# Making the context's gated convolution channels one stage earlier, on other engines

## The chip, the core and the metric

The kernel runs on one core of one Trainium2 chip. The core's engines work from queues of their own and wait for each other by semaphores: TensorE (PE, matrix products, with PEld for its weight loads), VectorE (DVE), ScalarE (ACT), GpSimd (POOL) and SyncE (SP, which here issues the loads). The metric is the device time of one execution in microseconds, lower is better.

## The reference, cut to what matters

Two blocks follow each other. The first one (two layers) ends with a feed-forward layer and a norm. The second one begins with the even mixer, which takes two streams of 256 tokens and 1024 channels: the latent stream, which is the first block's output, and the context stream, which is an input and depends on nothing before it.

```
p = h @ w_in                     # both streams, 2560 columns
a, gate = p[..., :512], p[..., 512:1024]
u = depthwise_conv(a * sigmoid(gate), conv_w (31 taps), conv_b)
conv = silu(layer_norm(u, ln_g, ln_b))
q, k, v = the other columns of p; attention over the keys of both streams
y = concat([conv, attention]) @ w_out
first block's last step:  x = x + 0.5 * (silu(gate) * up) @ w_down,  then a norm
```

## The kernel before

Activations lie with channels on the 128 partitions and tokens along the free axis. Every product is made in three passes: weights and activations are split into a rounded high part and a low rest, and `mm3` (L639 to L641) multiplies high by high, high by low and low by high. Weights come from DRAM in chunks of six 128x128 blocks (`raw`, issued by SP at L405); ACT makes the high part (`whi`, L418) and DVE the low one (`wlo`, L419, which reads `raw` and `whi`). Four buffers each of `raw`, `whi` and `wlo` let this run ahead of PE by at most three chunks; blocks are consumed in the order in which they were packed.

The feed-forward layer ahead of the even mixer (`ffn`, name `ffn2_1`) makes 22 pairs of products of its hidden units (gate and up, 8 blocks each, L715 to L719, split by L449 and L450) and then 8 products of 22 blocks, each of which is added to `x` (L725, L726) and fed to the next norms (`feed`: L478, L491, L492, L499 to L503). A generator `context` is woven into it (0.8 steps for each step of the layer): it loads nothing large, but sums, normalises and splits the context stream (L502, L520 to L524), so that the context is ready for products before the mixer starts.

The mixer (`even`) starts with four channel groups `m`. For each, `linc` makes the products of both streams from one pass over the weights: context first (256 columns, evacuated by ACT alone, L681), then latent (258 columns; these need the norm's factor `R`, which two reciprocals at L623 give some microseconds later: L685 on DVE, then L687, L688 on ACT). The gated unit goes to `glu[m]`, a tile with both streams side by side (L1161). The convolution of a group is a generator of 31 taps (`taps`), each 128x512, both streams at once. On DVE a tap is one SCALAR_TENSOR_TENSOR (L1092) into PSUM (`ms`); for groups marked otherwise ACT scales the shifted tile into `z` (L1089) and POOL adds `z` to `conv` (L1090). `BY` gives the engine of each group: 0 is DVE, 1 is ACT and POOL, -14 gives 14 taps to DVE and 17 to ACT and POOL. `tap` is called after each stream's products and hands out as many taps as `TAPS` says (first pair of numbers while the gated units are made, second pair in k, v and q). The k, v and q products follow (4 groups each, with a rotation of the latent k and q by a small matmul, L1182 to L1186, and transposes of v, L1196), then the attention (scores L1236, maxima L1238, exponentials L1241, transposes L1254 and L1256, values L1259, merge L1268 to L1281), into which `EV_FILL` weaves the q products, the rest of the convolution, its layer norm (`conv_norm`, L1310 to L1339) and the first output products.

The order of each engine's queue is set by a scheduler when the program is built; `issue_after(s.mark)` says that a tap stands behind the marked ACT instruction. At run time each queue goes strictly in its order.

Of the kernel before, what the change touches and what calls it, by code (L numbers as in the profile page):

```python
# [17 lines left out]
F32 = mybir.dt.float32  # L18
# [5 lines left out]
P = 128  # L24
# [22 lines left out]
TAPS = ((4.0, 4.0), (2.0, 2.0))  # L47
BY = (0, 1, 0, -14)
# [58 lines left out]
def _ffn_blocks(gu, down, parts):  # L107
# [195 lines left out]
def _prep(i):  # L303
# [4 lines left out]
    for l in range(2):  # L308
        for w in (1, 2):
            a[f"w_ffn{w}_{l}"] = _pack(_ffn_blocks(i[f"ffn{w}_w_gu"][l], i[f"ffn{w}_w_down"][l], FFN_PARTS[w, l]))  # L310
            cols.add(f"ffn{w}_norm{l}", i[f"ffn{w}_norm"][l])
# [260 lines left out]
class Net:  # L572
# [128 lines left out]
    def ffn(s, name, nr, nxt, parts):  # L701
# [3 lines left out]
        with s.tc.tile_pool(name=name, bufs=1) as pool:  # L705
            n = max(len(hs) for hs in parts)
            h = Split(pool.tile([P, n, T], F32R, name="hh"), pool.tile([P, n, T], F32R, name="hl"))
            for hs in parts:
                for m in range(len(hs)):
# [361 lines left out]

    def even(s, nrs, pool, cat, nxts):
# [3 lines left out]
        W31 = 31  # L1076
        cw, cb = s.col("ev_conv_w"), s.col("ev_conv_b")
        us, convs, due, ends = [], {0: [], 1: []}, {0: 0.0, 1: 0.0}, []

        def taps(u, y, m, by, js, last):  # L1080

            acc = y if by else s.ms().rearrange("p (s t) -> p s t", s=2)
            for j in js:
                k, v = cw[:, m * W31 + j:m * W31 + j + 1], u[:, :, j:j + T]
                if j == js[0]:
                    nc.scalar.activation(acc, v, AF.Copy, scale=k)
                elif by:
                    z = pool.tile([P, 2, T], F32, tag="w8", name="z", bufs=8)
                    nc.scalar.activation(z, v, AF.Copy, scale=k)  # L1089
                    nc.gpsimd.tensor_tensor(y, y, z, op=ALU.add)  # L1090
                else:
                    nc.vector.scalar_tensor_tensor(acc, v, k, acc, op0=ALU.mult, op1=ALU.add)  # L1092
                if j == js[-1]:
                    ends.append([2, lambda: last(acc)])
                yield

        def halve(y, m, acc):
            nc.scalar.activation(y, acc, AF.Identity, scale=0.5, bias=cb[:, m:m + 1])

        total = []  # L1100

        def done(y):

            total.append(y)
            if len(total) == 2:
                t = pool.tile([P, 2, T], F32, tag="w8", name="total", bufs=8)
                eng = nc.vector if len(us) == 4 and not any(convs.values()) else nc.gpsimd
                eng.tensor_tensor(t, total[0], total[1], op=ALU.add)
                total[:] = [t]

        def convolve(m, u):
            y = u[:, :, :T] if BY[m] == 0 else pool.tile([P, 2, T], F32, name=f"conv{m}")
            us.append(y)
            if BY[m] in (0, 1):
                convs[BY[m]].append(taps(u, y, m, BY[m], range(W31), lambda acc: (halve(y, m, acc), done(y))))
                return

            n, parts = -BY[m], []

            def part(acc):  # L1120
                parts.append(acc)
                if len(parts) == 2:
                    v = next(a for a in parts if a is not y)
                    t = pool.tile([P, 2, T], F32, tag="w8", name="z", bufs=8)
                    halve(t, m, v)
                    nc.vector.scalar_tensor_tensor(y, y, 0.5, t, op0=ALU.mult, op1=ALU.add)
                    done(y)

            convs[0].append(taps(u, None, m, 0, range(n), part))
            convs[1].append(taps(u, y, m, 1, range(n, W31), part))  # L1130

# [15 lines left out]

        glu = [pool.tile([P, 2, T + W31 - 1], F32, name=f"glu{m}") for m in range(4)]
        for u in glu:
            nc.gpsimd.memset(u[:, :, :15], 0.0)  # L1150
            nc.gpsimd.memset(u[:, :, 15 + T:], 0.0)
        for m in range(4):
            pa, pg = s.linc(w, nrs), s.linc(w, nrs)
            u = glu[m]
            for st in pa:
                a, th = pa[st], s.tmp("t3")
                if not nrs[st].full:
                    a = s.tmp("t2")
                    s.scaled(a, pa[st], nrs[st])
                s.scaled(th, pg[st], nrs[st], AF.Tanh, 0.5)  # L1160
                nc.vector.scalar_tensor_tensor(u[:, st, 15:15 + T], th, 1.0, a, op0=ALU.add, op1=ALU.mult)  # L1161
                tap(TAPS[0])
            convolve(m, u)
            yield
# [59 lines left out]
        def attend(st):  # L1224
# [5 lines left out]
            def probs(b, h):  # L1230
                es, r = [], s.tmp("mx", 8, bufs=6)
                assert {("q", h), ("v", h)} <= ready
                for mp in range(2):
# [6 lines left out]
                    e = pool.tile([P, S], F32, tag="e1" if st else "w8", name="e", bufs=4 if st else 8)  # L1240
# [63 lines left out]
        def conv_norm():  # L1304
# [3 lines left out]
            wide = lambda: pool.tile([P, 2, T], F32, tag="w8", name="wide", bufs=8)  # L1308
# [715 lines left out]
    def first_block(s):  # L2024
# [36 lines left out]
        drain(weave(s.ffn("ffn2_1", nr, nx, FFN_PARTS[2, 1]), ctx, 0.8))  # L2061
        drain(ctx)
# [34 lines left out]
```

## Time and profile before

| what | value |
|---|---|
| median of 3 runs (range) | 2242.39 us (2240.51 to 2242.43) |
| the profiled execution: its own time, its span | 2243.55 us, 2241.8 us |
| PE, DVE, ACT, POOL busy, share of the span | 98%, 77%, 57%, 4% |
| last feed-forward layer, some 984 to 1170 us: PE busy | 186.0 of 186 us |
| even mixer up to the attention, 1170 to 1290 us: PE and DVE busy | 113.6 and 104.7 of 120 us |
| attention to the first output products, 1290 to 1400 us: PE and ACT busy | 99.4 and 79.9 of 110 us |

PE is close to always busy, so time is to be won only where a stretch shows fewer matmuls than PE can start; the windows by stretch are the place to look, and after them the chain of waits there. Of a busy PE the number of instructions in a window tells more than the busy time. The clock that TensorE was granted stands in each window (1.00 is 2.4 GHz).

### The profile page before, as it was taken

The numbers are of one execution on the slowest core, as the hardware profiler recorded it, in microseconds if no ns is written. First come the engines' busy times: TensorE is split into PE (matmuls) and PEld (weight loads), VectorE is DVE, ScalarE is ACT, GpSimd is POOL, SyncE is SP. The second block draws the span as 40 slices with busy tenths as digits, with TensorE's granted clock in tenths as the row PEclk, the third lists the DMA queues.
The fourth block names the chain that finished last, engine by engine and source line by source line (L and its number), as shares of the span: only waits on it lengthen the run. The fifth ranks groups of instructions, "written<-read, shape, count | busy, mean of one in ns | idle before, by whom it ended". The sixth has DMA issues, their size and how long they took to land.

```text
span 2241.8 us, 43778 instructions
## 1 busy us (share of the span) xinstructions
PE 2194.7 (98%) x16832; PEld 2078.5 (93%) x16832; DVE 1715.6 (77%) x3322; ACT 1286.3 (57%) x2455; POOL 79.9 (4%) x116
## 2 busy tenths in 40 slices
PE   8999999999999999999999889999999999999998
PEld 8999999999999999999999857989989888999998
DVE  7877978887688778786768997767664779778565
ACT  6554666655555455675656677624435588437574
POOL 0000000000000000000004800000000000000000
PEclk9999999999999999999999989999999999999999
DMA  8776655776677756466662203456653325225564
GB/s 268 241 232 206 174 169 165 238 219 201 200 238 241 232 163 188 132 217 192 187 181 78 78 29 101 144 161 209 226 164 95 93 63 180 62 62 156 184 184 132
DMA packets 155755, 374.71 MB, mean 167 GB/s; under 512 B 24856, under 2 KB 29720, under 8 KB 155160
## 3 DMA queue, kind: packets, MB, share of 16 engines
q1 hardware_dynamic: 155544, 371.90, 53.5%
q8 instruction: 132, 2.16, 0.4%
q14 instruction: 79, 0.65, 0.1%
HBM read 365.81 MB, written 6.03 MB: 166 GB/s over the span
## 4 chain that ended last, share of the span: by engine, by line
PE 87%; DVE 6%; ACT 3%; DMA 2%; issue 1%; SPq 0%; DVEq 0%; ACTq 0%
PE mm L639 26%; PE mm L641 26%; PE mm L640 26%; DVE wlo L419 2%; DVE ms L1092 1%; PE ms L1610 1%; PE ms L1908 1%; PE mm L1883 1%; DMA raw<-w_mix 1%; PE ms L1701 1%; DMA raw<-w_ffn 1%; PE ms L1707 1%; ACT whi L418 0%; PE mm L1259 0%; PE mm L756 0%
## 5 line engine op out<-in xcount | busy, mean ns | idle before, releaser
L418 ACT ACTIVATE whi<-raw 128x768 fp32r<-128x768 f32 (+1 forms) x840 | 656.3, 786 | 652.6 <-PE mm L640 457.9
L639 PE MATMUL mm<-xh,whi 128*128 128x256 f32 (+1 forms) x3328 | 951.6, 286 | 10.8 <-ACT whi L418 10.0
L641 PE MATMUL mm<-xh,wlo 128*128 128x256 f32 (+1 forms) x3328 | 942.3, 284 | 5.8 <-DVE wlo L419 5.6
L640 PE MATMUL mm<-xl,whi 128*128 128x256 f32 (+1 forms) x3328 | 942.6, 283 | 0.0
L419 DVE TENSOR_TENSOR wlo<-raw,whi 128x768 fp32r<-128x768 f32 (+1 forms) x840 | 743.8, 894 | 257.5 <-ACT whi L418 253.3
L639 PEld LDWEIGHTS mm<-xh,whi 128*128 128x128 f32 x3328 | 632.0, 190 | 19.0 <-ACT whi L418 11.1
L641 PEld LDWEIGHTS mm<-xh,wlo 128*128 128x128 f32 x3328 | 632.7, 190 | 9.4 <-DVE wlo L419 8.9
L640 PEld LDWEIGHTS mm<-xl,whi 128*128 128x128 f32 x3328 | 632.3, 190 | 1.5 <-issue 0.3
L639 PE MATMUL mm<-hh,whi 128*128 128x256 f32 x704 | 198.0, 281 | 0.0
L641 PE MATMUL mm<-hh,wlo 128*128 128x256 f32 x704 | 197.7, 281 | 0.0
L640 PE MATMUL mm<-hl,whi 128*128 128x256 f32 x704 | 197.7, 281 | 0.0
L1002 DVE SCALAR_TENSOR_TENSOR junk<-adaw,cond 128x1024 bf16<-128x1024 f32 x160 | 194.8, 1217 | 1.1 <-DMA adaw<-adaT 0.9
L640 PE MATMUL mm<-ml,whi 128*128 128x512 f32 (+1 forms) x512 | 173.0, 338 | 0.0
L639 PE MATMUL mm<-mh,whi 128*128 128x512 f32 (+1 forms) x512 | 173.0, 338 | 0.0
L641 PE MATMUL mm<-mh,wlo 128*128 128x512 f32 (+1 forms) x512 | 173.0, 338 | 0.0
L639 PEld LDWEIGHTS mm<-hh,whi 128*128 128x128 f32 x704 | 132.8, 189 | 0.6 <-DVE wlo L419 0.2
L640 PEld LDWEIGHTS mm<-hl,whi 128*128 128x128 f32 x704 | 132.8, 189 | 0.1
L641 PEld LDWEIGHTS mm<-hh,wlo 128*128 128x128 f32 x704 | 132.7, 189 | 0.0
L641 PEld LDWEIGHTS mm<-mh,wlo 128*128 128x128 f32 x512 | 96.3, 188 | 11.7
L639 PEld LDWEIGHTS mm<-mh,whi 128*128 128x128 f32 x512 | 96.3, 188 | 11.6
L640 PEld LDWEIGHTS mm<-ml,whi 128*128 128x128 f32 x512 | 96.3, 188 | 11.5
L685 DVE TENSOR_TENSOR t<-mm,R 128x256 f32<-128x256 f32 x154 | 63.9, 418 | 28.7 <-PE mm L641 28.4
(513 smaller groups left out, 2924.0 us busy)
## 6 DMA issues: line engine op xcount, KB each, us to landing
raw<-w_ffn SPq DMA_DIRECT2D x352, 384.0 KB, 3.7
raw<-w_mlp SPq DMA_DIRECT2D x172, 384.0 KB, 3.2
raw<-w_mix SPq DMA_DIRECT2D x228, 256.0 KB, 2.8
adaw<-adaT SPq DMA_DIRECT2D x96, 512.0 KB, 4.0
raw<-w_od SPq DMA_DIRECT2D x50, 384.0 KB, 3.1
raw<-w_ev SPq DMA_DIRECT2D x38, 384.0 KB, 3.1
hyspec<-spec SPq DMA_DIRECT2D x10, 256.0 KB, 2.4
cond<-c SPq DMA_DIRECT2D x4, 512.0 KB, 6.0
```

The source lines that it names most:

```text
L418: nc.scalar.activation(hi[:, :w], raw, AF.Copy)
L419: nc.vector.tensor_sub(lo[:, :w], raw, hi[:, :w].bitcast(F32))
L639: mm(ps, whi, xhi, start=start, stop=False)
L640: mm(ps, whi, xlo, start=False, stop=False)
L641: mm(ps, wlo, xhi, start=False, stop=stop)
L685: nc.vector.tensor_mul(t, ps[:, :T], R)
L1002: nc.vector.scalar_tensor_tensor(junk, w, 1.0, cb[st], op0=ALU.mult, op1=ALU.mult, accum_out=s.mods[st, l][:, m:m + 1])
L1092: nc.vector.scalar_tensor_tensor(acc, v, k, acc, op0=ALU.mult, op1=ALU.add)
L1610: nc.tensor.transpose(v4(pt)[:, h], src[:, h], s.c("ident"))
L1701: mm(half(pz)[:, h], AT[:, h], first(X[:, h]), start=True, stop=True)
L1707: mm(half(pd)[:, h], XT[:, h], Z[:, h], start=True, stop=True)
L1883: nc.tensor.matmul(ps, dft[:, b, fs], zt[b], start=b == 0, stop=b == 1)
```

## The change

The context's half of the gated units and of the convolution leaves the mixer. The weights of the gated units are packed a second time into the stream of `ffn2_1`, behind the hidden units 12, 15, 18 and 21 (`SIDE`); there `context_glu` makes the context's two products of one group and its gated unit. From then on `context_taps` hands out eight of the context's taps (`CTAPS`) at each step of the layer, all four groups on ACT and POOL, 128x256 each. `context` is woven in at 1.5 steps instead of 0.8, so that the context is split by hidden unit 12. In the mixer the gated units are made for the latent stream alone, the taps are 128x256, groups 0 and 2 go to DVE and 1 and 3 to ACT and POOL, and `TAPS` is (8, 5) and (2, 3). The tag "w8" has seven buffers instead of eight, `z` has four of its own.

```diff
-TAPS = ((4.0, 4.0), (2.0, 2.0))
-BY = (0, 1, 0, -14)
+TAPS = ((8.0, 5.0), (2.0, 3.0))
+BY = (0, 1, 0, 1)
+SIDE = (12, 15, 18, 21)
+CTAPS = 8
...
             bl += (_late if m == 0 else _blocks)(gu, [m, NFF + m], range(KD))
+            if side is not None and m in SIDE:
+                i = SIDE.index(m)
+                bl += _blocks(side, [i, 4 + i], range(KD))
...
-                    nc.scalar.activation(t, g, AF.Silu)
+                    s.mark = nc.scalar.activation(t, g, AF.Silu).ins
                     s.last = nc.vector.tensor_mul(f, pu, t).ins
                     h.put(nc, m, f)
                     yield
+                    if side is not None and hs[m] in SIDE:
+                        side(w, SIDE.index(hs[m]))
...
+    def glued(s, m, st, pa, pg, nr):
+
+        th = s.tmp("t3")
+        if not nr.full:
+            a = s.tmp("t2")
+            s.scaled(a, pa, nr)
+            pa = a
+        s.scaled(th, pg, nr, AF.Tanh, 0.5)
+        s.nc.vector.scalar_tensor_tensor(s.glu[m][:, st, 15:15 + T], th, 1.0, pa, op0=ALU.add, op1=ALU.mult)
+
+    def taps(s, m, st, by, last):
+
+        nc, cw, u = s.nc, s.col("ev_conv_w"), s.glu[m][:, st]
+        acc = s.cv.tile([P, T], F32, tag="conv", name="conv", bufs=2) if by else s.ms()[:, :T]
+        for j in range(W31):
+            k, v = cw[:, m * W31 + j:m * W31 + j + 1], u[:, j:j + T]
+            if j == 0:
+                nc.scalar.activation(acc, v, AF.Copy, scale=k)
+            elif by:
+                z = s.cv.tile([P, T], F32, tag="z", name="z", bufs=4)
+                nc.scalar.activation(z, v, AF.Copy, scale=k)
+                nc.gpsimd.tensor_tensor(acc, acc, z, op=ALU.add)
+            else:
+                nc.vector.scalar_tensor_tensor(acc, v, k, acc, op0=ALU.mult, op1=ALU.add)
+            if j == W31 - 1:
+                last(lambda: nc.scalar.activation(u[:, :T], acc, AF.Identity, scale=0.5, bias=s.col("ev_conv_b")[:, m:m + 1]))
+            yield
+
+    def context_glu(s, w, m, nr):
+        pa, pg = s.linc(w, {1: nr})[1], s.linc(w, {1: nr})[1]
+        s.glued(m, 1, pa, pg, nr)
+        s.cconvs.append(s.taps(m, 1, 1, lambda f: f()))
+
+    def context_taps(s, n):
+        with s.tc.issue_after(s.mark):
+            for _ in range(n):
+                while s.cconvs and next(s.cconvs[0], 0) == 0:
+                    s.cconvs.pop(0)
+
...
-            pa, pg = s.linc(w, nrs), s.linc(w, nrs)
-            u = glu[m]
-            for st in pa:
...
-                tap(TAPS[0])
-            convolve(m, u)
+            pa, pg = s.linc(w, {0: nrs[0]})[0], s.linc(w, {0: nrs[0]})[0]
+            s.glued(m, 0, pa, pg, nrs[0])
+            tap(TAPS[0])
+            convolve(m)
...
-        drain(weave(s.ffn("ffn2_1", nr, nx, FFN_PARTS[2, 1]), ctx, 0.8))
-        drain(ctx)
+
+        def side(w, m):
+            drain(ctx)
+            s.context_glu(w, m, c1)
+
+        for _ in weave(s.ffn("ffn2_1", nr, nx, FFN_PARTS[2, 1], side), ctx, 1.5):
+            s.context_taps(CTAPS)
```

What the scheduler makes of it is seen at three places. The first is ACT's queue in the last feed-forward layer, late among the hidden units; before, it holds the splits, the SiLU (`t<-t`), the cast of the hidden unit (`hh`) and the context's normalisation (`t<-t,mods`, `xh`).

```order
L418 ACTIVATE whi<-raw 128x768 x2
L718 ACTIVATE t_14802<-t 128x256
L521 ACTIVATE t_14809<-t,mods_89 128x256
L523 CAST xh<-t_14809 128x256
L418 ACTIVATE whi<-raw 128x768
L449 CAST hh<-t_14803 128x256
L418 ACTIVATE whi<-raw 128x768 x2
```

Of the change, with a side product (its tanh is `t<-mm`) between two hidden units:

```order
L425 ACTIVATE whi<-raw 128x768 x4
L725 ACTIVATE t_14810<-t 128x256
L1108 ACTIVATE z<-glu_13501,cols 128x256 x3
L456 CAST hh<-t_14811 128x256
L1108 ACTIVATE z<-glu_13501,cols 128x256 x5
L425 ACTIVATE whi<-raw 128x768 x3
L688 ACTIVATE t_14902<-mm 128x256
L425 ACTIVATE whi<-raw 128x768 x2
L725 ACTIVATE t_14975<-t 128x256
```

Eight scalings for the convolution now stand between the splits of one hidden unit and those of the next; the context's normalisation has moved to earlier units. The second place is the same queue among the layer's last eight products, before (`sq`, `x` and `xh` are the norms' feed):

```order
L418 ACTIVATE whi<-raw 128x768 x4
L502 ACTIVATE sq<-x 128x256
L478 ACTIVATE x<-x,cols 128x256
L491 ACTIVATE xh<-x,mods_87 128x256
L502 ACTIVATE sq<-x 128x256
L418 ACTIVATE whi<-raw 128x768 x4
```

and of the change:

```order
L425 ACTIVATE whi<-raw 128x768
L1108 ACTIVATE z<-glu_13504,cols 128x256 x2
L425 ACTIVATE whi<-raw 128x768
L1108 ACTIVATE z<-glu_13504,cols 128x256 x3
L425 ACTIVATE whi<-raw 128x768
L1108 ACTIVATE z<-glu_13504,cols 128x256 x4
L425 ACTIVATE whi<-raw 128x768
L509 ACTIVATE sq<-x 128x256
L1108 ACTIVATE z<-glu_13504,cols 128x256
L485 ACTIVATE x<-x,cols 128x256
```

Each split there has come to stand behind two to four scalings. The third place is DVE's queue in the mixer while the k products are made, before (`kall` is the rotation, `t<-mm,R` the latent evacuation):

```order
L1185 TENSOR_TENSOR kall<-t_16736,c_ev 128x256
L1092 SCALAR_TENSOR_TENSOR ms<-glu_15948,cols,ms 128x512 x5
L1184 TENSOR_TENSOR t<-ms,c_ev 128x256
L685 TENSOR_TENSOR t<-mm,R 128x256
L1186 TENSOR_TENSOR kall<-kall,t 128x256
L419 TENSOR_TENSOR wlo<-raw,whi 128x768
```

and of the change:

```order
L1111 SCALAR_TENSOR_TENSOR ms<-glu_13501,cols,ms 128x256
L1193 TENSOR_TENSOR kall<-kall,t 128x256
L1111 SCALAR_TENSOR_TENSOR ms<-glu_13501,cols,ms 128x256
L692 TENSOR_TENSOR t<-mm,R 128x256
L1111 SCALAR_TENSOR_TENSOR ms<-glu_13501,cols,ms 128x256
L1111 SCALAR_TENSOR_TENSOR ms<-glu_13503,cols,ms 128x256
L1111 SCALAR_TENSOR_TENSOR ms<-glu_13501,cols,ms 128x256
L1111 SCALAR_TENSOR_TENSOR ms<-glu_13503,cols,ms 128x256
L426 TENSOR_TENSOR wlo<-raw,whi 128x768
```

The taps are as many up to the attention, half as wide, and stand more singly between the instructions that PE waits for.

## Rows read from the trace of the kernel before

**Rows 1.** The page, part 1: busy us (share of the span) and instructions.

```profile
span 2241.8 us, 43778 instructions
...
PE 2194.7 (98%) x16832; PEld 2078.5 (93%) x16832; DVE 1715.6 (77%) x3322; ACT 1286.3 (57%) x2455; POOL 79.9 (4%) x116
```

**Rows 2.** Windows by stage: PE, PEld, DVE, ACT, POOL busy, PEclk, DMA.

```profile
984.00:1170.00 186.00, 186.00 (x1564) 185.89 (x1564) 133.54 (x234) 116.41 (x195) 0.00 (x0) 1.00 0.63 195
1170.00:1290.00 120.00, 113.55 (x911) 112.23 (x910) 104.67 (x140) 74.28 (x142) 70.70 (x56) 0.97 0.27 83
1290.00:1400.00 110.00, 99.41 (x499) 72.19 (x498) 88.65 (x243) 79.94 (x194) 0.00 (x0) 0.94 0.20 63
```

**Rows 3.** Windows of 20 us in the mixer, same columns.

```profile
1100.00:1120.00 20.00, 20.00 (x170) 20.00 (x170) 12.52 (x21) 11.49 (x21) 0.00 (x0) 1.00 0.61 188
...
1240.00:1260.00 20.00, 16.41 (x113) 15.76 (x112) 19.64 (x28) 12.68 (x25) 16.10 (x13) 0.85 0.20 60
...
1300.00:1320.00 20.00, 18.53 (x97) 11.60 (x95) 19.65 (x65) 12.18 (x36) 0.00 (x0) 1.00 0.07 21
1320.00:1340.00 20.00, 13.38 (x65) 8.30 (x64) 16.07 (x53) 18.13 (x46) 0.00 (x0) 0.82 0.06 20
1340.00:1360.00 20.00, 18.14 (x83) 12.12 (x81) 16.01 (x46) 18.16 (x40) 0.00 (x0) 0.84 0.01 2
```

**Rows 4.** The chain that ended last, in the mixer: start us, us, what.

```profile
1229.36 2.83 DVE wlo L419 x2
1232.19 1.44 DVE kall L1185
...
1245.34 1.97 DVE wlo L419
...
1305.12 0.66 DVE ms L1092
```

**Rows 5.** Instructions of the convolution: min/median/max ns, first and last start us.

```profile
L1092 DVE SCALAR_TENSOR_TENSOR ms<-glu,cols,ms x73: 737/756/759, 1196.9 to 1310.4; 128x512 f32<-128x512 f32 x73
...
L1089 ACT ACTIVATE z<-glu,cols x46: 702/711/718, 1205.2 to 1282.0; 128x512 f32<-128x512 f32 x46
L1090 POOL TENSOR_TENSOR conv<-conv,z x46: 1259/1299/2057, 1206.0 to 1283.6; 128x512 f32<-128x512 f32 x46
```

**Rows 6.** The k and q rotations' first product (DVE, L1185), same columns.

```profile
L1185 DVE TENSOR_TENSOR kall<-t,c_ev x4: 411/1412/1512, 1232.1 to 1255.2; 128x256 f32<-128x256 f32 x4
L1185 DVE TENSOR_TENSOR q<-t,c_ev x4: 406/417/426, 1286.9 to 1306.1; 128x256 f32<-128x256 f32 x4
```

**Rows 7.** ACT, DVE, 1060 to 1170 us, by line: busy us, mean ns, idle, enders.

```profile
L418 ACT ACTIVATE whi<-raw 128x768 fp32r<-128x768 f32 x52 | 43.9, 844 | 39.1 <-PE mm L640 31.2 <-DVE wlo L419 3.9 <-issue 2.1
...
L419 DVE TENSOR_TENSOR wlo<-raw,whi 128x768 fp32r<-128x768 f32 x53 | 50.6, 957 | 22.5 <-ACT whi L418 22.3
...
L450 DVE TENSOR_TENSOR hl<-t,hh 128x256 fp32r<-128x256 f32 x9 | 3.8, 419 | 0.0
```

**Rows 8.** POOL by line, 1160 to 1400 us, same columns.

```profile
L1151 POOL MEMSET glu<- 128x30 f32 x4 | 0.5, 123 | 0.0
```

**Rows 9.** Timeline, ACT, kernel's start: start us, us, instruction, count.

```profile
8.74 2.51 ACT L491 ACTIVATE xh<-x,cols 128x256 fp32r<-128x256 f32 x6 [0.55 <-DMA x<-xT]
```

**Rows 10.** Timelines of POOL and DVE in the mixer.

```profile
1219.02 33.59 POOL L1090 TENSOR_TENSOR conv<-conv,z 128x512 f32<-128x512 f32 x22 [1.61 <-ACT z L1089]
...
1266.83 5.49 DVE L1092 SCALAR_TENSOR_TENSOR ms<-glu,cols,ms 128x512 f32<-128x512 f32 x7
```

**Rows 11.** Timelines of PE and DVE where the mixer starts.

```profile
1182.21 1.03 PE L547 MATMUL ms<-acc,consts 128*128 128x256 f32 x4
...
1191.88 1.08 DVE L685 TENSOR_TENSOR t<-mm,R 128x256 f32<-128x256 f32 x3
```

**Rows 12.** ACT by line, 1320 to 1360 us.

```profile
L622 ACT ACT_TABLE_LOAD x3 | 3.8, 1283 | 0.1
...
L1241 ACT ACT_TABLE_LOAD x3 | 3.8, 1283 | 0.1
```

More of the change, by code (lines that the diff above doesn't have):

```diff
@@ L45 @@
 ATV = 2
-TAPS = ((4.0, 4.0), (2.0, 2.0))
-BY = (0, 1, 0, -14)
+TAPS = ((8.0, 5.0), (2.0, 3.0))
+BY = (0, 1, 0, 1)
+SIDE = (12, 15, 18, 21)
+CTAPS = 8
+W31 = 31
 MW = 1
@@ L104, in _pack, with _ffn_blocks @@
     return out
-def _ffn_blocks(gu, down, parts):
+def _ffn_blocks(gu, down, parts, side=None):
     bl = []
@@ L309, in _prep @@
         for w in (1, 2):
-            a[f"w_ffn{w}_{l}"] = _pack(_ffn_blocks(i[f"ffn{w}_w_gu"][l], i[f"ffn{w}_w_down"][l], FFN_PARTS[w, l]))
+            side = i["ev_w_in_2"][0] if (w, l) == (2, 1) else None
+            a[f"w_ffn{w}_{l}"] = _pack(_ffn_blocks(i[f"ffn{w}_w_gu"][l], i[f"ffn{w}_w_down"][l], FFN_PARTS[w, l], side))
             cols.add(f"ffn{w}_norm{l}", i[f"ffn{w}_norm"][l])
@@ L698, in lin_tok, with ffn @@
         return pss
-    def ffn(s, name, nr, nxt, parts):
+    def ffn(s, name, nr, nxt, parts, side=None):
         nc = s.nc
@@ L1070, in even_shared @@
         s.vall = pool.tile([P, 4, 512], F32, name="vall")
+        s.glu = [pool.tile([P, 2, T + W31 - 1], F32, name=f"glu{m}") for m in range(4)]
+        for u in s.glu:
+            nc.gpsimd.memset(u[:, :, :15], 0.0)
+            nc.gpsimd.memset(u[:, :, 15 + T:], 0.0)
+        s.cv = pool
+        s.cconvs = []
+    def glued(s, m, st, pa, pg, nr):
[31 more added lines that the diff above has]
+                    s.cconvs.pop(0)
     def even(s, nrs, pool, cat, nxts):
@@ L1075, in even @@
         w = s.w.start("ev")
[L1076 to L1098, printed above, removed]
+        convs, due, ends = {0: [], 1: []}, {0: 0.0, 1: 0.0}, []
         total = []
@@ L1105, in done, with convolve @@
             if len(total) == 2:
-                t = pool.tile([P, 2, T], F32, tag="w8", name="total", bufs=8)
-                eng = nc.vector if len(us) == 4 and not any(convs.values()) else nc.gpsimd
+                t = pool.tile([P, 2, T], F32, tag="w8", name="total", bufs=7)
+                eng = nc.vector if not any(convs.values()) else nc.gpsimd
                 eng.tensor_tensor(t, total[0], total[1], op=ALU.add)
                 total[:] = [t]
[L1111 to L1130, printed above, removed]
+        us = [u[:, :, :T] for u in s.glu]
+        def convolve(m):
+            convs[BY[m]].append(s.taps(m, 0, BY[m], lambda f: ends.append([2, lambda: (f(), done(us[m]))])))
         def tap(n):
@@ L1145, in tap @@
                             c.pop(0)
[L1148 to L1151, printed above, removed]
+        while s.cconvs:
+            s.context_taps(1)
         for m in range(4):
-            pa, pg = s.linc(w, nrs), s.linc(w, nrs)
-            u = glu[m]
-            for st in pa:
[L1156 to L1161, printed above, removed]
-                tap(TAPS[0])
-            convolve(m, u)
+            pa, pg = s.linc(w, {0: nrs[0]})[0], s.linc(w, {0: nrs[0]})[0]
+            s.glued(m, 0, pa, pg, nrs[0])
+            tap(TAPS[0])
+            convolve(m)
             yield
@@ L1307, in conv_norm @@
                 yield
-            wide = lambda: pool.tile([P, 2, T], F32, tag="w8", name="wide", bufs=8)
+            wide = lambda: pool.tile([P, 2, T], F32, tag="w8", name="wide", bufs=7)
             mean = s.ms()
```

2 lines of the change are left out of this document (1 added, 1 removed).

## The prediction

> **What bounds the kernel now.** I read the page's part 1 first: PE is busy 98% of 2241.8 us, DVE 77%, ACT 57%, POOL 79.9 us in all [rows 1]. So only what PE does not use can be won, and any engine that makes PE late costs time. Next come the windows by stage, where the reader should look at the number of matmuls beside PE's busy time [rows 2]. At full rate PE starts 170 in 20 us [rows 3], 0.1176 us each. The feed-forward layer runs at that rate without a gap (186.0 of 186 us), with DVE at 133.5 and ACT at 116.4 us. The mixer up to the attention holds 911 matmuls in 120 us; 911 x 0.1176 = 107.2, so 12.8 us are missing. A little of that is matmuls in two passes (they are priced below with the norm's sums); **about 11 us are lost**. There DVE is busy 104.7 of 120 us, and in the worst 20 us it is busy 19.64 while PE starts 113 matmuls and the clock falls to 0.85 [rows 2, 3]. The chain that ended last runs over DVE in that place: low parts of weights and a rotation [rows 4]. Two things fill DVE: taps of 756 ns each, still in progress at 1310 us [rows 5], and work stretched by POOL: the rotation's product takes 411 ns at best but 1412 to 1512 while POOL adds, and 406 to 426 when POOL is done [rows 6]. From 1300 to 1360 us PE idles 1.5 + 6.6 + 1.9 = 10 us, at a clock of 0.82 and 0.84 in the last two windows, first beside a DVE busy 19.65 of 20, then beside an ACT busy 18.1 [rows 3].
>
> **The change part by part.** *PE's work is unchanged*: each stream has matmuls of its own, so 4 x 48 = 192 matmuls of the context, 192 x 0.1176 = 22.6 us, only move from the mixer to the layer. The weights of the gated units are loaded and split twice: 64 blocks, about 11 more chunks of six, 11 x 0.844 = 9.3 us on ACT and 11 x 0.957 = 10.5 us on DVE [rows 7], in a stage where both have room (70 and 52 us) and DMA is busy 0.63 [rows 2]. I cost this and SP's 11 loads at nothing beside PE; without that cover it would be up to 10.
>
> *The feed-forward layer (a loss).* 120 adds of 128x256 on POOL and their scalings on ACT enter a stage that has no POOL work. No row shows such an add. Half of the 1259 ns at 512 columns [rows 5] is 0.63; with the 123 ns of the smallest POOL instruction as fixed part [rows 8] it is 0.123 + 0.568 = 0.69; if the columns did not count at all it would be 1.26, which the 123 ns speak against. I take 0.66. A scaling of 128x256 is 2.51 / 6 = 0.42 [rows 9]. Eight of each per step stand beside one hidden unit, 48 matmuls or 5.65 us. ACT alone has 8 x 0.42 + 2.67 x 0.844 + about 1 for SiLU and cast = 6.6 there, but the side products bring PE time without taps; beside a last product (66 matmuls, 7.76 us) it has 3.36 + 3.67 x 0.844 + 4 x 0.42 = 8.1. Both are a little too much, for steps that its lead of three chunks (3 x 18 x 0.1176 = 6.4 us) can bridge.
>
> The sharper limit is POOL against DVE. While POOL adds, DVE instructions with two inputs in SBUF are late [rows 6], and POOL itself loses: 22 adds took 33.59 us [rows 10], 5.9 more than 22 x 1.259. In those 33.59 us PE made some 255 matmuls [rows 2], 36 to a chunk, so DVE made 7 low parts, 6.8 us: about 0.85 of DVE's two-input time was added to POOL's. In the layer the taps cover nine hidden units with three side products (12 x 5.65 = 67.8 us of PE) and 6.5 last products (50.4 us), 118 us. POOL needs 120 x 0.66 = 79; DVE's two-input work there is 56 low parts x 0.957 + 9 x 0.419 [rows 7] = 57. With 0.85 of it, 79 + 48 = 127, **10 us more than PE's**. This becomes PE's wait because `z` has four buffers and ACT's queue runs in order: a scaling that waits for POOL holds up the splits `whi` behind it, and `wlo` and PE behind these. Before, `whi` itself waits for PE to give buffers back (31.2 us [rows 7]), so the first 6.4 us may be absorbed: lower bound 10 - 6.4, about 4. Upper bound: exclusion in full, step by step, without averaging. Three units and a side product need 24 x 0.66 + 10.7 x 0.957 + 1.3 = 27.3 against 22.6 of PE, 4.7 over, three times; a last product 5.3 + 3.5 + 0.4 = 9.2 against 7.76, 1.5 over, 6.5 times: 24. I take 10, from the nearest row [rows 10].
>
> The Trainium skill ("SBUF — State Buffer", section "Who interferes with whom") states this as a rule against the change: GpSimd and a DVE operation with two SBUF inputs share one port pair, and whoever starts first holds it for its whole instruction. The 411 and 1512 ns agree in kind; by the rule taken in full the layer would lose 24 instead of 10, and the change would lose 9 instead of gaining 5.
>
> *The mixer up to the attention (a gain).* DVE makes 60 of its taps here, as before, but of 256 columns: I take 0.42, as a product of that size [rows 6], instead of 0.756 (in a quiet stretch 5.49 / 7 = 0.78 [rows 10]), so 60 x 0.34 = 20 us less, and 1.7 less for four gated products: 104.7 - 22 = 83. POOL's adds go from 46 x 1.30 = 60 us [rows 5] to 60 x 0.66 = 40, so about a third of the stretching (some 15 us, mostly rotations and low parts) goes too: 77. PE keeps 107.2 - 22.6 = 84.6 and is again the longer one. POOL's 40 plus 0.85 of DVE's two-input work fits in that. Of the 11 lost us I keep 3: **gain 8**. Bounds: 11 (PE never waits) and 4, because DVE at 77 of 85 us is nearly as full as before and its queue is in order. With the context gone, less PE work stands ahead of the latent evacuation, which begins 8.6 us after the norm's sums end [rows 11] (four matmuls in 1.03 us, 0.14 each over the usual; a dozen of their kind make the 2 us that I kept out of the 11); five PSUM buffers of products (15 us of PE) lie between, so I cost it at up to 1, inside the 3.
>
> *The attention (a gain).* 73 - 60 = 13 DVE taps of 0.66 to 0.76, 9 to 10 us, leave 1290 to 1310, where DVE is full and one tap is on the chain [rows 3 to 5]. The convolution's norm can begin some six steps earlier; its ACT work, with table loads of 1.28 each way [rows 12], moves from windows where ACT is at 18.1 into one where it is at 12.2 [rows 3]. Of PE's 10 idle us there I take back **7**; bounds 2 (softmax alone holds PE) and 12 (the clock comes back too).
>
> Sum: + 10 - 8 - 7 = - 5 on the profiled execution's 2243.55, which gives 2238.5. The median of the runs is 1.2 below that execution, so 2237.
>
> **The rivals.**
>
> 1. *Slower: POOL and DVE exclude each other in the layer.* If steps can't borrow from each other, + 24 - 15 = + 9: 2251. For it: the 1512 ns and four buffers of `z`. Against it: 31.2 us in which `whi` now waits for PE. It decides as soon as the layer gives back over 15 + 4.5 = 20 us, which is also reached if an add takes 0.75 or more (+ 0.09 x 120 = 11 on the 10).
> The Trainium skill ("GPSIMD Engine Reference", section "3.1 Elementwise — side-by-side cycle accounting") gives 4497 ns for an fp32 add of 2048 columns; with the trace's 1259 at 512 an estimate for 256 is 720 ns, by which the layer would lose about 7 more. No run here has shown that size.
> 2. *No change: the layer gives back what the mixer and the attention gain*, 13 to 15 each: 2242. For it: ACT's own load beside the last products, 8.1 against 7.76.
> 3. *A larger gain: the layer hides it all.* The lead and the side products' PE time absorb the excess: 0 - 15 gives 2227. For it: DVE and ACT have 52 and 70 us of room in that stage. Against it: POOL's 127 against 118.
> 4. *It doesn't do what it says:* taps stand singly between what PE waits for, DVE stays the mixer's bound, the gain is 4 + 2 and the loss 10: 2246.
>
> **How the numbers follow.** About 0.2% (4.5 us) is what a measurement tells from no change here. My forecast, a gain of 5 (-1 to -11), gets 0.38; rival 3 gets 0.13, rival 2 0.16, rival 4 0.10, rival 1 0.23. Faster by over 0.2%: rival 3 and about 0.30 of the forecast's 0.38, 0.43. Slower: rival 1 and 0.04 of rival 4, 0.27. The rest, 0.30, is within. The range reaches from just below rival 3 (2224) to rival 1 (2252); add times near 1 us lie outside. The forecast's own range is 2231 to 2241.
>
> **What would show it.** In the layer: the mean of the adds (0.66 or 0.75 and more) and of `wlo` (0.957, or stretched well beyond); matmuls per 20 us below 170 from the first side product on; the chain there going over `z` and POOL instead of PE. In the mixer: 719 matmuls in about 88 us, taps at 0.42, rotations less often at 1.4. In the attention: no tap after the first scores, PE above 18 us in each window of 20. The prediction is wrong if the layer keeps 170 matmuls per 20 us (then it is faster than I say), or if PE's gaps there add up to more than 20 us, or if PE is as far from its matmuls' time in the mixer as before.

## The result and the profile after

The changed kernel takes 2283.0 us (median of 4 runs, 2277.7 to 2285.8) against 2242.4; the ratio is 1.0177 [1.0154, 1.0200]. It is slower by 1.8%, outside the range and on the other side of the forecast. Its span of 2282.5 us is 40.7 longer than that of [rows 1], with the same 16832 PE instructions:

```profile
span 2282.5 us, 44226 instructions
...
PE 2209.2 (97%) x16832; PEld 2085.1 (91%) x16832; DVE 1708.7 (75%) x3319; ACT 1338.8 (59%) x2607; POOL 178.0 (8%) x250
```

Since PE does the same work, four places of the program that stand in both kernels cut the difference into stages. For the kernel before, by line (min/median/max ns, first and last start): the casts of hidden units, the last layer's products, the scores, the attention's products with the values.

```profile
L449 ACT CAST hh<-t x22: 386/392/408, 997.4 to 1109.6; 128x256 fp32r<-128x256 f32 x22
...
L641 PE MATMUL mm<-hh,wlo x176: 277/281/283, 1108.3 to 1170.6; 128*128 128x256 f32 x176
...
L1236 PE MATMUL ms<-kall,q x32: 376/376/480, 1290.7 to 1352.7; 64*128 64x256 f32 x32
...
L1259 PE MATMUL mm<-vall,pT x96: 271/275/508, 1308.1 to 1366.0; 128*128 128x128 f32 x96
```

The same rows of the changed kernel:

```profile
L456 ACT CAST hh<-t x22: 387/391/409, 1003.4 to 1151.0; 128x256 fp32r<-128x256 f32 x22
...
L648 PE MATMUL mm<-hh,wlo x176: 277/281/393, 1156.7 to 1229.1; 128*128 128x256 f32 x176
...
L1243 PE MATMUL ms<-kall,q x32: 376/480/792, 1319.1 to 1392.5; 64*128 64x256 f32 x32
...
L1266 PE MATMUL mm<-vall,pT x96: 272/275/581, 1338.7 to 1408.9; 128*128 128x128 f32 x96
```

**The layer** (first cast to last product): 225.7 against 173.2 us, + 52.5, of which 22.6 are the moved products: **29.9 lost**. **The mixer** up to the first score: 90.0 against 120.1, and 22.6 of the difference is moved work: **7.5 gained**. **The attention** (first score to last product with the values): 89.8 against 75.3: **14.5 lost**. The first cast is 6.0 us late already, in a part where both programs are the same (in the other runs below it is -1.6 to + 5.2 from that of before: executions differ by that much), and behind the attention 2.2 are gained: 6.0 + 29.9 - 7.5 + 14.5 - 2.2 = 40.7.

In the layer, windows of 20 us (columns as in [rows 2]) show where it begins:

```profile
1060.00:1080.00 20.00, 20.00 (x171) 20.00 (x170) 11.05 (x18) 12.81 (x24) 4.66 (x6) 1.00 0.55 162
1080.00:1100.00 20.00, 17.74 (x143) 16.93 (x142) 11.83 (x13) 14.13 (x28) 16.25 (x18) 1.00 0.47 137
1100.00:1120.00 20.00, 16.43 (x122) 15.60 (x121) 10.66 (x16) 14.59 (x32) 13.85 (x16) 0.92 0.47 141
...
1140.00:1160.00 20.00, 15.58 (x123) 14.76 (x123) 11.94 (x16) 15.95 (x35) 15.90 (x19) 1.00 0.46 135
```

PE makes 171 matmuls until POOL's first taps and 122 to 143 beside them, and no engine is full: DVE 11 to 12, ACT 14 to 16, POOL 14 to 16 of 20. Four engines wait for each other in turn. By line, 1070 to 1215 us (columns as in [rows 7]):

```profile
L1109 POOL TENSOR_TENSOR conv<-conv,z 128x256 f32<-128x256 f32 x120 | 111.7, 931 | 115.4 <-ACT z L1108 106.9
...
L426 DVE TENSOR_TENSOR wlo<-raw,whi 128x768 fp32r<-128x768 f32 x53 | 62.5, 1199 | 44.9 <-ACT whi L425 44.9
...
L1108 ACT ACTIVATE z<-glu,cols 128x256 f32<-128x256 f32 x120 | 56.2, 501 | 15.8 <-POOL conv L1109 15.5
```

An add takes 0.93 us on the mean, a low part 1.20 where it took 0.957 [rows 7], and ACT, which stood idle because PE had no free buffers [rows 7], now stands 15.5 us for POOL. The two collide: all 35 adds of more than 1.25 us overlap in time with a DVE instruction with two inputs in SBUF, and all 36 low parts of more than 1.0 us overlap with an add, of the 30 shorter ones only 7 (1060 to 1230 us). PE's own waits (us in total, times, longest), 1000 to 1225 us, are half for the high parts and half for the low ones:

```profile
PE mm L646 <- ACT whi L425: 10.5, 10, 2.4
PE mm L648 <- DVE wlo L426: 10.4, 16, 1.6
```

That is some 21 of the 29.9 us; the rest lies inside PE's busy time (1099 matmuls in 138.8 us from 1070 to 1229, 0.126 each instead of 0.1176). The chain of waits goes round that ring, 39% of it over POOL's adds (start us, us, what):

```profile
1111.09 0.41 ACT z L1108
1111.94 0.47 issue
1112.44 0.74 POOL conv L1109
...
1116.55 1.32 POOL conv L1109
1117.95 1.34 POOL conv L1109
...
1123.25 0.84 ACT whi L425
1124.15 0.71 issue
1125.15 1.50 DVE wlo L426
1126.67 5.19 DMA raw<-w_ffn
```

Adds of 0.74, then two of 1.3 beside DVE's low parts; the split that stood behind the scalings in ACT's queue; a low part of 1.50 beside an add; then a load of weights of 5.19 us, for which the next split waits. It is the only load of note on the chain (3.6% of 1078 to 1222 us), but it shows that the ring can also go over the weights' buffers.

In the mixer, its 90 us, the taps on DVE, and the first product of a rotation (which answers to [rows 6]):

```profile
1229.00:1319.00 90.00, 86.47 (x705) 85.13 (x704) 72.32 (x132) 65.55 (x151) 54.59 (x61) 1.00 0.38 114
```

```profile
L1111 DVE SCALAR_TENSOR_TENSOR ms<-glu,cols,ms x60: 472/484/492, 1251.9 to 1306.7; 128x256 f32<-128x256 f32 x60
...
L1192 DVE TENSOR_TENSOR kall<-t,c_ev x4: 418/492/1004, 1265.9 to 1287.6; 128x256 f32<-128x256 f32 x4
```

PE is the longer one again (86.5 against 72.3 of DVE), at full clock. In the attention, windows and the middle of the chain:

```profile
1340.00:1360.00 20.00, 16.55 (x67) 9.38 (x66) 15.28 (x51) 12.26 (x30) 0.00 (x0) 0.83 0.00 0
1360.00:1380.00 20.00, 15.89 (x71) 10.68 (x70) 14.38 (x40) 18.14 (x47) 0.00 (x0) 0.91 0.00 1
1380.00:1400.00 20.00, 14.19 (x67) 9.66 (x67) 12.36 (x38) 13.43 (x32) 0.00 (x0) 0.83 0.13 40
```

```profile
1364.54 0.70 ACT wide L1341
1365.24 0.70 ACT wide L1342
...
1371.69 0.51 ACT cath L1345
1372.56 0.51 ACT cath L1345
...
1381.76 1.28 ACT L1248
1383.06 0.78 ACT e L1248 x2
1384.15 3.14 PE mm L1266 x12
```

From 1364 to 1373 ACT makes the last part of the convolution's norm almost in one piece while exponentials and copies wait behind it; PE idles 3.5, 4.1 and 5.8 us in three windows where before it idled 6.6 and 1.9 in two [rows 3], at a granted clock of 0.83 to 0.91 (0.82 and 0.84 before). Over the whole stretch PE idles 14.7 us against 10.0, and it is busy 75.1 us with 367 matmuls against 65.4 with 347, at 0.89 against 0.91. So a third of the 14.5 is idle time; which matmuls make up the rest was not followed.

### The profile page after: what moved, and what is told of

Same layout as the page of the kernel before. It is cut to its first block, busy times and chain, and to the rows that moved or that the text cites. A ratio compares the mean times of both kernels' runs of the same rounds, so it can differ in the third digit from the quotient of the medians.

```text
span 2282.5 us, 44226 instructions
## 1 busy us (share of the span) xinstructions
PE 2209.2 (97%) x16832; PEld 2085.1 (91%) x16832; DVE 1708.7 (75%) x3319; ACT 1338.8 (59%) x2607; POOL 178.0 (8%) x250
## 4 chain that ended last, share of the span: by engine, by line
PE 79%; ACT 6%; DVE 5%; POOL 3%; DMA 3%; issue 2%; SPq 0%; POOLq 0%; DVEq 0%; ACTq 0%
PE mm L648 23%; PE mm L646 23%; PE mm L647 23%; POOL conv L1109 3%; DVE wlo L426 2%; ACT whi L425 2%; DMA raw<-w_ffn 1%; DMA raw<-w_mix 1%; PE ms L1617 1%; PE ms L1915 1%; PE mm L1890 1%; PE ms L1708 1%; PE mm L1266 1%; PE ms L1714 1%; PE mm L765 0%
## 5 line engine op out<-in xcount | busy, mean ns | idle before, releaser
L426 DVE TENSOR_TENSOR wlo<-raw,whi 128x768 fp32r<-128x768 f32 (+1 forms) x851 | 759.3, 902 | 283.9 <-ACT whi L425 279.5
L1109 POOL TENSOR_TENSOR conv<-conv,z 128x256 f32<-128x256 f32 x180 | 165.0, 917 | 163.7 <-ACT z L1108 151.0
```

Of the source, the lines that this page charges most:

```text
L426: nc.vector.tensor_sub(lo[:, :w], raw, hi[:, :w].bitcast(F32))
L1109: nc.gpsimd.tensor_tensor(acc, acc, z, op=ALU.add)
```

## The experiments

"Lost" is worked out as above (11.3 us of moved work in e9), for the hidden units (first cast to the first of the layer's last products, 1108.0 before), the last products, the mixer and the attention; negative is gained. Each figure is of one execution. The layer of the change, which stands unaltered in e1, e7 and e8, lost 29.9, 28.6, 29.9 and 30.3 us, so differences of 1 to 2 us mean nothing. e2, e3 and e11 to e14 make another convolution of the context.

| kernel | us | ratio to before | units | last products | mixer | attention |
|---|---|---|---|---|---|---|
| the change | 2283.0 | 1.0177 [1.0154, 1.0200] | 19.8 | 10.1 | -7.5 | 14.5 |
| e1_pad6 | 2265.4 | 1.0102 [1.0083, 1.0122] | 18.4 | 10.2 | -7.4 | 0.1 |
| e2_no_adds | 2249.4 | 1.0036 [1.0021, 1.0051] | 1.9 | -0.1 | -7.4 | 13.1 |
| e3_one_scaling | 2297.8 | 1.0254 [1.0233, 1.0274] | 14.4 | 33.9 | -7.4 | 12.5 |
| e4_z8 | 2273.3 | 1.0146 [1.0122, 1.0170] | 13.4 | 10.7 | -7.4 | 14.2 |
| e5_slower_taps | 2266.6 | 1.0107 [1.0091, 1.0123] | 1.4 | 11.2 | 9.0 | 1.7 |
| e6_one_on_dve | 2254.1 | 1.0050 [1.0037, 1.0063] | 1.9 | 13.1 | -6.5 | 0.2 |
| e7_pad3 | 2274.8 | 1.0146 [1.0132, 1.0161] | 29.9 in all | | -7.3 | 13.0 |
| e8_pad9 | 2275.7 | 1.0153 [1.0136, 1.0170] | 30.3 in all | | -7.4 | 12.8 |
| e9_two_groups | 2255.6 | 1.0060 [1.0046, 1.0073] | 1.3 | 5.2 | 5.4 | 1.7 |
| e10_early | 2257.7 | 1.0068 [1.0055, 1.0080] | 6.1 | 9.2 | -0.4 | 0.1 |
| e11_memsets | 2237.1 | 0.9971 [0.9962, 0.9980] | 2.5 | -0.1 | -7.4 | 0.2 |
| e12_long_memsets | 2240.1 | 0.9988 [0.9977, 0.9998] | 4.0 | 0.0 | -7.5 | 0.8 |
| e13_memsets_as_adds | 2241.8 | 0.9992 [0.9981, 1.0002] | 6.0 | -0.1 | -7.4 | -0.4 |
| e14_memsets_as_late_adds | 2245.1 | 1.0008 [0.9998, 1.0017] | 3.5 | 6.0 | -6.8 | 0.2 |

**The attention: e1, e7, e8.** Six empty steps (three, nine) at the head of the convolution's norm:

```diff
             while any(convs.values()) or ends:
                 tap((1.0, 1.0))
                 yield
+            for _ in range(6):
+                yield
             wide = lambda: ...
```

> The change with six empty steps at the head of the convolution's norm, so that the table of fill steps in the attention meets the same work at the same place as before the change (before it, six steps of the fill handed out the last taps; now there are none left and everything behind moves up). In the changed kernel first score to last attention product takes 89.8 us against 75.3 before. Theory A (the table of fill steps is six steps out): the 89.8 fall to 68 to 77, the whole run to 2264 to 2271. Rival B (seven buffers instead of eight of the tag w8 hold up the exponentials): they stay at 88 to 91, the run at 2281 to 2285. The layer before it is not touched: its last product still starts some 36 us later than before the change, after the 22.6 us of moved products are taken off.

> As the kernel with six empty steps, but three. From first score to last attention product: 89.8 us with none, 75.4 with six, 75.3 before the change. Theory A (the work behind the convolution runs beside other attention work than the table was made for, and most of the loss comes from a few collisions): 78 to 86. If the taps that were at that place before the change are what cost 10 us there, less than 75 should be reached somewhere between none and six: 70 to 74 here. The layer ahead is as with six: a loss of 28.

> As the kernel with six empty steps, but nine. Theory A: the norm of the convolution and the output products behind it come three steps too late, so PE has less to fill with in the middle and more at the end: 77 to 84 us from first score to last attention product, against 75.4 with six. Rival: any later place is as good, since the taps are gone and nothing else changed: 74 to 76.

With six steps, scores and last product with the values:

```profile
L1243 PE MATMUL ms<-kall,q x32: 376/428/480, 1312.4 to 1374.5; 64*128 64x256 f32 x32
...
L1266 PE MATMUL mm<-vall,pT x96: 270/275/507, 1331.1 to 1387.8; 128*128 128x128 f32 x96
```

1387.8 - 1312.4 = 75.4 us, as before the change to 0.1, with seven buffers of "w8": theory A holds and B falls. Three and nine steps give 88.3 and 88.1, worse than A expected (78 to 86 and 77 to 84) and almost as bad as none: of the four places tried, the table fits one. What PE waits for says the same: ACT's copies of the transposed exponentials (`pT`) hold it up 6.7, 10.0 and 9.4 us with no, three and nine steps, and 0.4 with six. And nothing is gained at that place by the 13 DVE taps that have gone: with them and without them the stretch takes the same time.

**The layer, which partner: e2, e3, e4.** In turn, the adds left out, the scalings left out, eight buffers:

```diff
-                nc.gpsimd.tensor_tensor(acc, acc, z, op=ALU.add)
+                if st == 0 or j == 1:
+                    nc.gpsimd.tensor_tensor(acc, acc, z, op=ALU.add)
```

```diff
+                if st == 0 or j == 1:
                     z = s.cv.tile([P, T], F32, tag="z", name="z", bufs=4)
                     nc.scalar.activation(z, v, AF.Copy, scale=k)
```

```diff
+                if st:
+                    s.nz = getattr(s, "nz", -1) + 1
+                    z = s.kall[:, s.nz // 2 % 4, s.nz % 2 * T:s.nz % 2 * T + T]
...
```

> The change, with 29 of 30 of the context's adds on GpSimd left out (one per group is kept); ScalarE's scalings all stay. It computes another convolution of the context. The layer loses 31 us of PE time in the changed kernel. Theory L (ScalarE's queue stands behind GpSimd's chain of adds and PE behind ScalarE) and theory X (DVE and GpSimd hold each other up): the loss falls to 0 to 4, the last product of the layer starts at 1198 to 1203 us instead of 1228.8, the run at 2250 to 2256. Rival C (ScalarE has too much work of its own with 120 scalings): 12 to 25 us of the loss stay, 2264 to 2276.

> The change, with one scaling per group of the context instead of 30: GpSimd makes all 120 adds, but of the same tile. It computes another convolution of the context. GpSimd's adds now run freely and nothing on ScalarE waits for a buffer of them. Theory L: the layer's loss of 31 us falls to 2 to 7 (only low parts of weights that are late behind adds), the adds follow each other at 0.8 us and 1.4 where DVE holds them up, run 2254 to 2260. Theory X (mutual exclusion with DVE is what costs, with or without ScalarE's wait): 15 us or more stay, 2267 or more. Rival C (ScalarE's work): 0 to 4 stay.

> The change with eight buffers for the context's scaled tiles instead of four (slices of the keys' tile, which is empty at that time); nothing is left out. A step's eight scalings then fit without waiting for an add. Theory L, if the four buffers are the link: GpSimd's idle time inside the 120 adds, about 20 us, goes, the layer's loss falls from 31 to 8 to 14, run 2264 to 2272. If GpSimd's own pace (111.8 us busy plus 8.5 between adds, against 110.8 us of PE work in the same stretch) is already the bound behind it, no more than these 20 can go. Theories X and C: the loss stays at 28 to 33, run 2280 to 2286.

Without the adds 1.8 of 29.9 us stay: the moved products, the second loading of their weights and 120 scalings on ACT are nearly free; C falls. With the adds alone the loss doesn't fall but grows, to 48.3: L and C fall in their simple form, and X, which had said 15 or more, doesn't explain the growth. GpSimd now ran without a pause, as its timeline shows, 30 adds in 31 us, and ACT's next stop was the halving of the group's sum, which waits for the last of them:

```profile
1072.26 31.53 POOL L1110 TENSOR_TENSOR conv<-conv,z 128x256 f32<-128x256 f32 x30 [86.46 <-ACT z L1109]
1108.06 31.16 POOL L1110 TENSOR_TENSOR conv<-conv,z 128x256 f32<-128x256 f32 x30 [4.26 <-ACT z L1109]
```

```profile
1103.83 0.51 ACT L1114 ACTIVATE glu<-conv,cols 128x256 f32<-128x256 f32 x1 [8.92 <-POOL conv L1110]
```

The four halvings stood 8.9, 10.5, 19.8 and 20.1 us, the last two beside the last products, where the loss grew and where PE waited 27.3 us for high parts. So which instruction of ACT's queue waits doesn't matter, as long as one stands there that needs GpSimd to be through. Eight buffers give back 6 of 30, between what L (17 to 23) and X (none) had said: the buffers are a small part of it.

**The layer, how many adds: e5, e6, e9, e10**, all with the norm of the convolution at its old place.

```diff
-CTAPS = 8
+CTAPS = (5, 7)
...
+        for n, _ in enumerate(weave(s.ffn("ffn2_1", nr, nx, FFN_PARTS[2, 1], side), ctx, 1.5)):
+            s.context_taps(CTAPS[n >= NFF])
...
-        while s.cconvs:
-            s.context_taps(1)
+        convs[1] += s.cconvs
```

That is e5 (with four taps instead of three in `TAPS[1]` for ACT and POOL). In e6 it is (6, 8), and group 0 goes to DVE by a list of its own, two taps a step:

```diff
+        (s.cconvs if m else s.dconvs).append(s.taps(m, 1, min(m, 1), lambda f: f()))
...
+            s.context_taps(s.dconvs, 2)
+            s.context_taps(s.cconvs, CTAPS[n >= NFF])
```

In e9 it is (5, 3), SIDE = (12, 16), and the mixer makes groups 2 and 3 for both streams; in e10 (6, 3), SIDE = (7, 10, 13, 16), and 2.6 steps of `context`:

```diff
-            pa, pg = s.linc(w, {0: nrs[0]})[0], s.linc(w, {0: nrs[0]})[0]
-            s.glued(m, 0, pa, pg, nrs[0])
-            tap(TAPS[0])
+            these = {0: nrs[0]} if m < len(SIDE) else nrs
+            pa, pg = s.linc(w, these), s.linc(w, these)
+            for st in pa:
+                s.glued(m, st, pa[st], pg[st], nrs[st])
+                tap(TAPS[0])
```

> The change with the six empty steps, and with the context's taps handed out five at a hidden unit and seven at a last product instead of eight at both; what is left (some 15 to 25 taps of the last group) goes to GpSimd in the mixer, which hands out four taps there instead of three. The layer still loses 28 us with the six empty steps alone. Theory P (ScalarE's queue runs in order, and so a step of the layer can't end before GpSimd is through most of that step's adds; one add takes 0.81 us from start to start, about 1.0 with those that DVE holds up, so eight take 6.5 to 8.0 us beside a hidden unit of 5.65): five adds take 4.1 to 5.0 and seven 5.7 to 7.0 beside 7.76, so the loss falls to 2 to 8 and the run to 2240 to 2248. Theory X (it is the sharing of DVE's time with GpSimd that costs, by the number of adds): about 105 of 120 adds stay in the layer, so the loss stays at 22 to 26, run 2258 to 2264.

> The change with the six empty steps, and with one of the context's four groups on DVE, two taps at each step of the layer; the other three stay on ScalarE and GpSimd, six adds at a hidden unit, eight at a last product, 90 in all. Theory P: six adds take 4.9 to 6.0 us beside 5.65, eight 6.5 to 8.0 beside 7.76, so the loss falls from 28 to 4 to 10, run 2241 to 2248. A rival (DVE becomes the layer's bound: low parts, splits and norms of about 4.1 us a hidden unit, 0.96 more of taps and what GpSimd adds to it): the loss stays at 12 us or more, with PE waiting for low parts alone, run 2250 or more. Theory X (by the number of adds): 28 x 90 / 120 = 21, run 2258.

> Half of the change: the context's products, gated units and taps of groups 0 and 1 alone are made in the layer (behind hidden units 12 and 16), five taps at a hidden unit and three at a last product, on ScalarE and GpSimd; groups 2 and 3 stay in the mixer with both streams in one tap of 512 columns, as before the change. The norm of the convolution meets the table of fill steps at its old place (six steps). Theory P+X (beside a hidden unit the number of adds per step decides, beside a last product each add makes DVE's two-input work late): the units lose 0 to 1, the last products, with three adds each instead of seven or eight, 2 to 5 of the 11 to 14 they lost; the mixer gains about half of 7.4; run 2240 to 2246. Theory P alone: the last products lose 0 to 1, run 2237 to 2241.

> All four groups, but earlier: side products behind hidden units 7, 10, 13 and 16 (the context is normalised at 2.6 steps for each step of the layer instead of 1.5), six taps at a hidden unit, three at a last product, the rest (some 10 to 15) in the mixer. The table of fill steps is met at its old place. Theory P+X: the units lose 2 to 6 (six adds take 4.9 to 6.0 us beside 5.65, and the context's norm now stands closer), the last products 2 to 5; the mixer gains 3 to 7; run 2239 to 2250. A rival (the pull of the context's norm into the first units costs more than it frees): the stretch ahead of the first side product loses 5 us or more, where it lost 2.

Five adds per hidden unit cost 1.4 us, six 1.9 (e6), eight 18.4; without adds (e2) it was 1.9, so five or six are free. The six of e10 seem to cost 6.1, but 4.1 of these are lost in the 32 us from the first cast on, before its first add (237 matmuls where the kernel before makes 272), as its context's norm stands closer there. And the five are free although DVE is held up as before: e5's low parts take 1.21 us beside the units (1070 to 1133 us). Late low parts alone cost no time there; they do when the step's adds leave no room. Beside the last products it is otherwise: fewer adds there (seven for e5, three for e9 and e10) still lose 11.2, 5.2 and 9.2. Two windows of e5, hidden units and last products:

```profile
1075.00:1095.00 20.00, 20.00 (x171) 20.00 (x170) 14.82 (x20) 15.01 (x31) 10.03 (x12) 1.00 0.63 198
...
1155.00:1175.00 20.00, 17.10 (x124) 16.29 (x125) 18.05 (x19) 17.38 (x37) 18.59 (x19) 0.91 0.41 127
```

Beside the last products DVE makes `x`, `xl` and `acc` too, with two inputs in SBUF each, and is at 18.05 of 20. P's condition alone, seven adds in less than 7.76 us, doesn't save that stretch. In e6, with taps on DVE as well, the rival came true as written: 15.0 us lost, PE waiting 8.7 us for low parts and 0.6 for high ones beside the last products. None of the four wins: what leaves the layer comes back in the mixer, where 83 adds instead of 60 cost e5 16 us, where e10 keeps 0.4 of the 7.4 gained, and where e9's two groups of 512 columns with my division of taps are slower by 5.4 than before the change; e6 keeps its mixer and loses by its last products.

**The layer, occupation or collision: e11 to e14**, all as e1, with six empty steps. The adds give way to memsets of the scaled tile, which read nothing (28 of 30 in a group):

```diff
-                nc.gpsimd.tensor_tensor(acc, acc, z, op=ALU.add)
+                if st == 0 or j in (1, W31 - 1):
+                    nc.gpsimd.tensor_tensor(acc, acc, z, op=ALU.add)
+                else:
+                    for c in (T, T):
+                        nc.gpsimd.memset(z[:, :c], 0.0)
```

The widths are (T, T) in e11, (T, T, 100) in e12, (T, T, T) in e13, (T, T, T, 200) in e14.

> The kernel with six empty steps, in which 28 of 30 of the context's adds of a group are replaced by two GpSimd memsets of the scaled tile, 128x256 each (0.31 us by a row of the same shape later in the kernel, some 0.77 with the gaps, against 0.81 for an add from start to start). It computes another convolution of the context. GpSimd is occupied as long as by undisturbed adds, and ScalarE waits for it in the same way, but it reads no SBUF. Theory X (adds and DVE's two-input work hold each other up): the layer's loss of 30 us falls to 2 to 7, the last products lose 0 to 2 of their 10.8, low parts take 0.96 as without GpSimd; run 2238 to 2245. Theory P (GpSimd's occupation per step, through ScalarE's queue): beside the hidden units 8 x 0.77 = 6.2 against 5.65, three of four steps; 10 to 18 us of the loss stay, run 2247 to 2257.

> As the kernel with two memsets per tap, with a third of 100 columns, so that a tap takes GpSimd about 1.0 us, which is what an add and the time that DVE held it up took on the mean in the changed kernel (120 in 120 us). It computes another convolution of the context. Theory P: beside the hidden units 8 x 1.0 = 8 against 5.65 (with the side products 24 against 22.6 in three units), beside the last products 8 against 7.76; GpSimd's 120 us bind the layer as with adds, 12 to 20 us of the 30 are lost, nearly all of it ScalarE's splits coming late; run 2248 to 2258. Theory X: nothing is lost without reads on GpSimd, 2 to 6, run 2238 to 2244.

> As the kernel with two memsets per tap, with three of 256 columns. Memsets that follow each other start 0.27 us apart, so the two and the three of the runs before occupied GpSimd for 0.55 and 0.67 us per tap; three of 256 columns take 0.82, the pace of adds that nothing holds up (0.81). It computes another convolution of the context. Theory P (occupation of GpSimd alone): eight take 6.5 us beside a hidden unit of 5.65, so 4 to 8 us are lost beside the units, 0 to 1 beside the last products (6.5 against 7.76); with the rest of the layer 6 to 11 of the 28.6 us, run 2241 to 2248. Theory X (reads of SBUF on both sides): 2 to 4 lost in all, run 2237 to 2241.

> As the kernel with three memsets of 256 columns per tap, and a fourth of 200: about 1.04 us per tap, the mean pace of adds in the changed kernel, those that DVE held up among them (120 in about 120 us). It computes another convolution of the context. If ScalarE's wait for GpSimd at that pace is the way in which the time is lost, eight take 8.3 us beside a hidden unit of 5.65 (67 taps, 70 us, beside 62 us of PE with the side products) and 8.3 beside a last product of 7.76: 8 to 18 us lost beside the units, 2 to 5 beside the last products, waits for splits of ScalarE alone and low parts at 0.96; run 2249 to 2262. If late low parts on DVE are the way, 2 to 4 lost, run 2237 to 2241.

e11 and e12 told less than they were meant to, since memsets of 0.31 us start some 0.27 apart and occupied GpSimd for 0.55 and 0.67 us a tap. e14 is the one to read, 1070 to 1215 us by line:

```profile
L1113 POOL MEMSET z<- 128x256 f32 x336 | 93.1, 314 | 5.2 <-ACT z L1108 4.2
L1113 POOL MEMSET z<- 128x200 f32 x112 | 30.0, 267 | 0.5
...
L426 DVE TENSOR_TENSOR wlo<-raw,whi 128x768 fp32r<-128x768 f32 x64 | 61.2, 960 | 48.3 <-ACT whi L425 48.3
```

and its timeline of GpSimd, 85 memsets without a gap, 0.98 us for the four of a tap:

```profile
1071.85 20.74 POOL L1113 MEMSET z<- 128x256 f32 x85
```

GpSimd is as full as with adds, ACT waits for it, yet low parts stay at 0.960 us and the layer loses 9.5 us, at about the pace of undisturbed adds (e13) 5.9. P had said 10 to 23 and 6 to 11 for these two, X 2 to 4 for both; neither is right alone. So of e1's 28.6 us about 2 are the moved work, 4 to 8 GpSimd's time through ACT's queue, and the other 19 to 23 come only with real adds. An add differs from memsets in its length and in the chain through one accumulator as well as in its reads; that the reads do it, DVE and GpSimd holding each other up, is argued from the low parts, 1.20 us beside adds and 0.960 beside memsets, and from the overlaps above. Both theories had a part; X has the larger one, where adds leave a step no room (e5).

## Why the prediction was wrong

- **PE's work unchanged, weights loaded twice at nothing:** right. 16832 matmuls in both, and 1.8 us lost in e2.
- **The layer, + 10:** the term that failed first; 29.9 measured, beyond the upper bound of 24. I had the right partners, and the sum of work was, if anything, too high: GpSimd was busy for 111.7 us, about 120 with the gaps between adds, where I had 127 against PE's 118. What failed is "with 0.85 of it, 79 + 48 = 127", the whole stretch taken as one pool of time, and the allowance that "the first 6.4 us may be absorbed". Steps lent each other little time across this ring of queues in order: the step-by-step bound of 24 was the estimate to take. An add was also dearer than the 0.66 that I took: 0.73 us, and 0.81 from one start to the next. With 0.73 the same bound comes to about 32 (19 beside the units and 13 beside the last products), where 19.8 and 10.1 were measured. The Trainium skill ("GPSIMD Engine Reference", section "3.1 Elementwise — side-by-side cycle accounting") had given 720 ns by my estimate from it, nearer than my own.
- **The rule against the change** is borne out in kind: adds took 0.73 or 1.33 us, low parts 1.20 beside them, and 0.96 beside memsets, which read no SBUF. The rule stands in the Trainium skill ("SBUF — State Buffer", section "Who interferes with whom"). Its section "SBUF: two separate sides" limits the lock, for a DVE operation with two SBUF inputs, to GpSimd operations that read SBUF; e14 agrees. By the rule taken in full I had 24, nearer to 29.9 than my 10.
- **The mixer, - 8:** right, - 7.5, and PE is the longer one again as forecast: DVE at 72.3 of 90 us, PE at 86.5. Part of the agreement is luck: taps took 0.484 for the assumed 0.42, POOL was busy for 54.6 us, not 40.
- **The attention, - 7:** wrong in sign, + 14.5. "The convolution's norm can begin some six steps earlier" was right as a fact; counting it as a gain was the error. The table of fill steps had fitted that work to the scores. Moved up, the norm occupies ACT for 9 us where exponentials are due, and the first output products are made from 1368 to 1377 us, before the last scores (to 1392.5) need cover; right behind them PE stands 4.4 us for a copy of ACT. And the tap that I saw on the chain was not what held PE up: e1 has no taps there and takes 75.4 us, as before the change.
- **The rivals:** rival 1's mechanism, with late low parts on top of full steps, decided the layer, as said there beyond 20 us; it had a chance of 0.23 and a price of 24. No rival had the attention in it, which is half as much again.

A version that beats the kernel before wasn't found. e11, at 0.9971 without the context's convolution, shows how little there would be to win with this division: the mixer's 7.5 us, less about 2.

## What to carry to other kernels

Work that goes into a stage without gaps must fit step by step, not on the mean, when its engines wait for each other in queues of fixed order; and GpSimd adds beside DVE work with two SBUF inputs cost both engines their time. Where a table written by hand fits work to steps, count the steps that a change takes out ahead of it, and put empty ones in their place first.

## What the runs showed of the hardware

An add of 128x256 on GpSimd takes 0.73 us, or about 1.33 when it meets a DVE instruction with two inputs in SBUF for long (in the layer, 60 of 120 took under 0.76 and 33 took 1.25 to 1.40); a memset of that size takes 0.31 but follows the one ahead 0.25 us later within a tap, while adds into one tile start 0.08 us behind the end of the last.
